# State-space mixer: the pooled product as one float32 matmul, outputs ahead of injections, low parts between parts of a rotation

## The chip, the cores and the metric

The kernel runs on one core of a Trainium2 chip. The metric is device time in microseconds (us) of one execution. Three executions of the kernel before gave 1857.22, 1857.31 and 1859.56 us; the median is 1857.31. Engines are called by their short names: PE (TensorE, matmuls), DVE (VectorE), ACT (ScalarE), POOL (GpSimd) and SP (SyncE, which here only issues DMAs).

## The reference

A trunk of two layers over 512 tokens of 1024 channels, in float32. The change touches one stage of layer 0, the mixer. Its input projection gives 512 pooling channels and 512 state-space channels.

```python
def pool_mixer(u, w_grp, scale):          # 4 groups of 128 channels, windows 2, 4, 8, 16
    ...
        outs.append((csg[:, end] - csg[:, start]) / cnt - uf[:, :, c0:c1])
    p = jnp.stack(outs, axis=2)
    y = jnp.einsum('blgc,gcd->blgd', p, w_grp.astype(F32)).reshape(bsz, L, D_POOL)
    return (y * scale.astype(F32)).astype(u.dtype)

def s5_mixer(u, a_re, a_im, log_dt, b_re, b_im, c_re, c_im, d_skip, w_glu, b_glu):
    ...
    y = jnp.transpose(y_f + y_b, (1, 0, 2, 3)).reshape(bsz, L, D_SSM) + d_skip.astype(F32) * uf
    y = jax.nn.gelu(y)
    y = y * jax.nn.sigmoid(y @ w_glu.astype(F32) + b_glu.astype(F32))
    return y.astype(u.dtype)
```

`y_f` and `y_b` come from a complex diagonal recurrence forwards and backwards over the tokens. The two halves of the mixer are joined and multiplied by one output matrix (1024 x 1024, `ab_w_out`).

## The kernel before, in words

**Products in parts.** Nearly every large product is three matmuls (`mm3`, L179 to L183): a float32 operand is kept as a high part (a cast by ACT) and a low part (operand minus high part, by DVE), and the three are high by high, low by high, high by low. A weight comes from memory as `w_raw` (two buffers), is cast by ACT to `w_hi` (L124) and its low part is taken by DVE as `w_lo` (L135). `take()` hands over the next weight, `done()` gives one back and starts the cast and low part of the next ones. All loads of weights and tables are issued by SP in program order. A result of PE is split on its way out by `split_evac`: high part by ACT (L399), low part by DVE (L400).

**The mixer's stage** is the 136 us from 405 to 541 us of the span. Its 512 state-space channels are worked in four tiles `ct`. For each: `inject(ct)`, 64 small float32 matmuls into the one buffer `ps_x` (L1433); `scan(ct)`, all on DVE: two products of `ps_x` with a rotation `ce` (L1451, L1452, the "first pair"), an addition and a subtraction (L1454, L1455), four recurrences (L1460), two more rotation products (L1462, L1463) and four combinations (L1468); `permute(ct)`, two copies by ACT; `output(ct)`, 96 small matmuls into `ps_y` (L1490, L1494), a gelu by ACT (L1497) and a write to memory (L1498, ACT's queue); `y_rows(ct)`, the read of it in another layout (L1502, SP's queue); `split_y(ct)` (L1506, L1507). `scan` is a generator: at each `yield` the program may place other work before DVE's next part.

**The pooling half** has four tiles too. `pool_tile(i)` projects 128 channels (24 matmuls into the one buffer `ps_p`), ACT copies them out twice (`pz`, `pp`), and POOL forms the window sums, corrects the edges and subtracts (L1526 to L1537). `rest()` splits the result (L1541 ACT, L1542 DVE) and `pool_out(i)` multiplies it by a 128 x 128 weight in three matmuls; tiles 0 to 2 use the three `ps_A` banks, tile 3 uses `ps_p`.

**The output product** `out_a` adds up into `psA[0..3]`: the first three take over the three `ps_A` banks, so each waits until the pooled result in its bank has been evacuated. It also works in row parts: pooled channels first (`kt` 0 to 3), state-space channels later. After the four `y` tiles have arrived comes `glu` (three-part products into `psG`), then the loop over `d` (sigmoid by ACT L1645, product by DVE L1646, split L1649 and L1650), then the rest of `out_a`, and `psB`, the second half of the output columns.

What sets the order on an engine is the program alone: each engine executes its own instructions in the order in which the code was written, and waits at an instruction until its inputs are there and its output buffer is free.

Of the kernel before, what the change touches and what calls it, by code (L numbers as in the profile page):

```python
# [7 lines left out]
F32 = mybir.dt.float32  # L8
F32R = mybir.dt.float32r
# [6 lines left out]
P = 128  # L16
# [157 lines left out]
class Builder:  # L174
# [1199 lines left out]
    def mixer(self, nxt, before):  # L1374
# [43 lines left out]
        yp = y = yhl = sp = us = edge = None  # L1418
# [18 lines left out]
        def decay(ct):  # L1437
            rho = con[ct, "rho"] = sp.tile([P, 2, 4, 64], F32, tag="rho", bufs=2, name="rho")
            for d in range(2):
                col = 16 * d + 4 * ct  # L1440
                nc.scalar.copy(rho[:, d], self.rho8[:, col:col + 4].unsqueeze(2).broadcast_to([P, 4, 64]))
                nc.scalar.mul(rho[:, d, :, 63 * d:63 * d + 1], rho[:, d, :, 63 * d:63 * d + 1], 0.0)

        def scan(ct):
# [17 lines left out]
            V.tensor_tensor(out=t2, in0=t1, in1=rot(1), op=ALU.mult)  # L1462
            V.tensor_tensor(out=t1, in0=t1, in1=rot(0), op=ALU.mult)  # L1463
# [40 lines left out]
        def split_y(ct):  # L1504
            hi, lo = (z[:, ct] for z in yhl)
            nc.scalar.copy(hi, y[:, ct])  # L1506
            V.tensor_tensor(out=lo, in0=y[:, ct], in1=hi.bitcast(F32), op=ALU.subtract)  # L1507

        def pool_tile(i):
# [41 lines left out]
        lhs = lambda kt: (xh[:, kt], xl[:, kt])  # L1551
# [10 lines left out]
        for i, win in enumerate(self.POOL_W):  # L1562
            G.tensor_scalar(out=scol[:, i:i + 1], in0=scol[:, i:i + 1], scalar1=1.0 / win, scalar2=None, op0=ALU.mult)
        rest = [pool_tile(0)]
        decay(0)
        decay(1)
# [4 lines left out]
        rest.append(pool_tile(1))  # L1571
        rest[0]()
        decay(2)
        inject(1)
        load("m3", "e2")
        for _ in scan(1):
            pass
        rest.append(pool_tile(2))
        rest[1]()
        permute(0)  # L1580
        decay(3)
        inject(2)
        load("i1", "g1")
        self.W.done()
        output(0)
        turn = scan(2)
        next(turn)
        rest[2]()
        self.W.done()
        y_rows(0)  # L1590
        load("e3", "g2")
        for _ in turn:
            pass
        rest.append(pool_tile(3))
        permute(1)
        inject(3)
        output(1)
        load("i2")
        y_rows(1)
        load("g3", "i3")  # L1600
        w_pool = self.W.take()
        for i in range(3):
            pool_out(i)
        turn = scan(3)
        next(turn)
        rest[3]()
        self.W.done()
        permute(2)
        out_a(range(3), range(2))
        next(turn)  # L1610
        pool_out(3)
        for _ in turn:
            pass
        output(2)
        permute(3)
        split_y(0)
        split_y(1)
        out_a(range(3), range(2, 4))
        y_rows(2)
        self.W.done(2)  # L1620
        output(3)
        y_rows(3)
        wide = self.bank("ps_x")
        psG = [wide[:, :512], wide[:, 512:], self.bank("ps_p")]
        wG = [self.W.take() for _ in range(2)]

        def glu(ds, kts):
            for kt, d in [(kt, d) for kt in kts for d in ds]:
                if d == len(psG):
                    psG.append(self.bank("ps_y"))  # L1630
                self.mm3(psG[d], [z[:, kt % 2 * HALF + d * P:kt % 2 * HALF + (d + 1) * P] for z in wG[kt // 2]],
                         [z[:, kt] for z in yhl], kt == 0, kt == 3)

        glu(range(3), range(2))
        split_y(2)
        glu((3,), range(2))
        out_a((3,), range(2))
        self.W.done()
        glu(range(4), (2,))
        split_y(3)  # L1640
        glu(range(4), (3,))
        out_a((3,), range(2, 4))
        for d in range(4):
            s = sp.tile([P, SEQ], F32, tag="yt", bufs=2, name="sg")
            nc.scalar.activation(out=s, in_=psG[d], func=AF.Sigmoid, bias=bcol[:, d:d + 1])  # L1645
            V.tensor_tensor(out=y[:, d], in0=y[:, d], in1=s, op=ALU.mult)  # L1646
            nat = lambda z: z[:, 4 + d].rearrange("p (c j) -> p j c", j=8)
            src = y[:, d].rearrange("p (j c) -> p j c", j=8)
            nc.scalar.copy(nat(xh), src)  # L1649
            V.tensor_tensor(out=nat(xl), in0=src, in1=nat(xh).bitcast(F32), op=ALU.subtract)  # L1650
            if d == 1:
                self.W.done()
        self.W.done(2)
# [29 lines left out]
    def mid_weights(self, ly):  # L1683
        w = self.ins
        if ly == 0:
            l = [w["w_in"][i] for i in (4, 5, 6, 7, 0, 1, 2, 3)] + [w["w_pool"]]
# [105 lines left out]
def lay_out(inputs):  # L1792
# [26 lines left out]
    edge = np.zeros((4, 16), np.float32)  # L1819
    for i, w in enumerate(Builder.POOL_W):  # L1820
        edge[i, :w // 2] = [w / (t + w // 2) for t in range(w // 2)]
        edge[i, 8:7 + w // 2] = [w / (w - 1 - k) for k in range(w // 2 - 1)]
# [17 lines left out]
        "w_pool": np.concatenate([a["pool_w"][0].transpose(1, 0, 2).reshape(P, HALF),  # L1840
                                  np.zeros((P, HALF), np.float32)], axis=1),
# [30 lines left out]
```

## Time and profile before

| | |
|---|---|
| median of 3 executions | 1857.31 us |
| profiled execution | 1861.19 us |
| its span on the core | 1859.3 us |
| granted TensorE clock, mean | 0.990 |
| PE busy | 97 % |
| DVE busy | 80 % |
| ACT busy | 50 % |
| POOL busy | 19 % |

The profiled execution is one execution with the hardware profiler on; the span is the part of it from the first to the last instruction, and 1.9 us lie outside. Busy shares are means over all stages. In the mixer's stage they are others, and the times in it are read from the engines' timelines (start and duration of each instruction, in us from the span's start).

### The profile page before, as it was taken

How to read it: one execution, taken by the hardware profiler on the slowest of the kernel's cores; microseconds unless marked ns; L12 is line 12 of the kernel's file. 1: busy time of each engine (PE TensorE's matmuls, PEld its weight loads, DVE VectorE, ACT ScalarE, POOL GpSimd, SP SyncE). 2: the span in 40 equal slices, each digit the busy share in tenths (PEclk: the TensorE clock that was granted, in tenths of full speed). 3: DMA queues.
4: the chain of work that ended last, by engine and by line, in shares of the span. 5: the costliest groups of instructions: out<-in, count | busy, mean ns of one | idle time of the engine just before them, and what ended most of it. 6: DMA issues, size and time to landing. Idle time of an engine off the chain costs nothing.

```text
span 1859.3 us, 31315 instructions
## 1 busy us (share of the span) xinstructions
PE 1798.2 (97%) x12144; PEld 1626.2 (87%) x12144; DVE 1486.4 (80%) x2396; ACT 935.7 (50%) x1769; POOL 360.9 (19%) x254
## 2 busy tenths in 40 slices
PE   8999999998899999999999999999999899999998
PEld 7887997787679999988899998889888789999886
DVE  6898989968769999854799997455887589999745
ACT  6254446355456444444644445346777464454532
POOL 1021321014111322300123221002333012223100
PEclk9999999999999999999999999999999899999999
DMA  5474346638532333232223333323333223332331
GB/s 198 137 222 165 103 135 193 207 123 261 176 114 81 102 113 103 92 125 92 90 92 103 113 103 115 101 69 109 112 110 105 89 80 103 103 111 95 125 102 58
DMA packets 88932, 224.42 MB, mean 121 GB/s; under 512 B 16560, under 2 KB 29008, under 8 KB 87760
## 3 DMA queue, kind: packets, MB, share of 16 engines
q1 hardware_dynamic: 77088, 196.75, 32.3%
q0 software_dynamic: 6960, 23.57, 4.2%
q10 hardware_dynamic: 4736, 2.10, 0.4%
q8 instruction: 96, 1.57, 0.4%
q14 instruction: 52, 0.43, 0.1%
HBM read 205.64 MB, written 18.84 MB: 121 GB/s over the span
## 4 chain that ended last, share of the span: by engine, by line
PE 59%; DVE 9%; ACT 3%; issue 2%; DMA 2%; POOL 0%; DVEq 0%; ACTq 0%; POOLq 0%
PE ps_gu L183 10%; PE ps_gu L182 10%; PE ps_gu L181 10%; PE ps_A L181 3%; PE ps_A L183 3%; PE ps_A L182 3%; PE ps_B L181 3%; PE ps_B L183 3%; PE ps_B L182 3%; PE ps_f L181 2%; PE ps_f L183 2%; PE ps_f L182 2%; DVE w_lo L135 2%; ACT junk L237 1%; PE ps_o L958 1%
## 5 line engine op out<-in xcount | busy, mean ns | idle before, releaser
L135 DVE TENSOR_TENSOR w_lo<-w_raw,w_hi 128x1024 fp32r<-128x1024 f32 x214 | 283.0, 1327 | 211.6 <-ACT w_hi L124 211.2
L124 ACT CAST w_hi<-w_raw 128x1024 fp32r<-128x1024 f32 (+1 forms) x313 | 262.9, 864 | 279.2 <-PE ps_A L183 74.1
L183 PE MATMUL ps_gu<-xsum,w_lo 128*128 128x256 f32 x1088 | 308.9, 284 | 0.8 <-DVE w_lo L135 0.8
L182 PE MATMUL ps_gu<-xsum,w_hi 128*128 128x256 f32 x1088 | 308.6, 284 | 0.8 <-DVE xsum L518 0.8
L183 PE MATMUL ps_gu<-xT_hi,w_lo 128*128 128x256 f32 (+1 forms) x1008 | 307.6, 305 | 1.7 <-DVE w_lo L135 1.7
L181 PE MATMUL ps_gu<-xsum,w_hi 128*128 128x256 f32 x1088 | 308.3, 283 | 0.0
L181 PE MATMUL ps_gu<-xT_hi,w_hi 128*128 128x256 f32 (+1 forms) x1008 | 304.9, 302 | 0.0
L182 PE MATMUL ps_gu<-xT_lo,w_hi 128*128 128x256 f32 (+1 forms) x1008 | 304.6, 302 | 0.0
L183 PEld LDWEIGHTS ps_gu<-xsum,w_lo 128*128 128x128 f32 x1088 | 209.4, 192 | 1.0 <-DVE w_lo L135 0.9
L182 PEld LDWEIGHTS ps_gu<-xsum,w_hi 128*128 128x128 f32 x1088 | 209.2, 192 | 1.0 <-DVE xsum L518 1.0
L181 PEld LDWEIGHTS ps_gu<-xsum,w_hi 128*128 128x128 f32 x1088 | 209.1, 192 | 0.0
L183 PEld LDWEIGHTS ps_gu<-xT_hi,w_lo 128*128 128x128 f32 x1008 | 190.4, 189 | 14.2 <-DVE w_lo L135 3.4
L181 PEld LDWEIGHTS ps_gu<-xT_hi,w_hi 128*128 128x128 f32 x1008 | 190.3, 189 | 8.5 <-issue 0.9
L182 PEld LDWEIGHTS ps_gu<-xT_lo,w_hi 128*128 128x128 f32 x1008 | 190.2, 189 | 7.3
L109 POOL TENSOR_TENSOR w_u<-w_raw,w_s 128x512 f32<-128x512 f32 x64 | 112.2, 1753 | 354.7 <-ACT w_hi L124 196.0
L124 ACT CAST w_hi<-w_s 128x512 fp32r<-128x512 f32 x136 | 77.8, 622 | 197.4 <-DVE w_s L105 197.4
L135 POOL TENSOR_TENSOR w_lo<-w_raw,w_hi 128x1024 fp32r<-128x1024 f32 x31 | 74.2, 2395 | 497.4 <-ACT w_hi L124 469.1
L105 DVE TENSOR_TENSOR w_s<-w_raw,w_u 128x1024 f32<-128x1024 f32 x68 | 145.8, 2144 | 2.3
L640 POOL TENSOR_TENSOR g<-g,m 128x1024 f32<-128x1024 f32 x34 | 94.6, 2782 | 244.9 <-DVE m L638 244.9
L181 PE MATMUL ps_B<-w_hi,gT 128*128 128x512 f32 x352 | 137.8, 391 | 2.0 <-DVE free L1303 2.0
L183 PE MATMUL ps_A<-w_hi,gT 128*128 128x512 f32 x352 | 137.7, 391 | 1.1 <-DVE gT L693 1.1
L181 PE MATMUL ps_A<-w_hi,gT 128*128 128x512 f32 x352 | 138.1, 392 | 0.0
(381 smaller groups left out, 4215.5 us busy)
## 6 DMA issues: line engine op xcount, KB each, us to landing
w_raw<-in_w_gu_dram SPq DMA_DIRECT2D x106, 512.0 KB, 3.4
w_raw<-in_w_dn_dram SPq DMA_DIRECT2D x88, 512.0 KB, 3.3
w_u<-in_w_gu_dram SPq DMA_DIRECT2D x70, 512.0 KB, 3.7
w_raw<-in_w_qk_dram SPq DMA_DIRECT2D x16, 512.0 KB, 3.4
w_raw<-in_w_in_dram SPq DMA_DIRECT2D x8, 512.0 KB, 3.4
cm<-m_dram SPq DMA_DIRECT2D x4, 1024.0 KB, 8.3
w_raw<-in_w_ao_dram SPq DMA_DIRECT2D x8, 512.0 KB, 3.8
cg<-g_dram SPq DMA_DIRECT2D x4, 1024.0 KB, 7.2
```

The source lines that it names most:

```text
L105: tt(out=blocks(s), in0=g[:, :HALF].unsqueeze(1).broadcast_to([P, 2, HALF]), in1=blocks(u)[:, :2], op=ALU.subtract)
L109: (h_engine or self.nc.gpsimd).tensor_tensor(out=z["h"], in0=g[:, HALF:], in1=z["s"][:, HALF:], op=ALU.add)
L124: self.nc.scalar.copy(hi[:, k:k + step], src[:, k:k + step])
L135: (engine or self.lo_engine).tensor_tensor(out=lo[:, :n], in0=src, in1=hi[:, :n].bitcast(F32), op=ALU.subtract)
L181: mm(ps, a[0], b[0], start=start, stop=False)
L182: mm(ps, a[0], b[1], start=False, stop=False)
L183: mm(ps, a[1], b[0], start=False, stop=stop)
L237: self.nc.scalar.activation(out=junk[:, :src.shape[-1]], in_=src, func=AF.Square, scale=scale, accum_out=out)
L640: nc.gpsimd.tensor_tensor(out=rows(f), in0=rows(f), in1=m, op=ALU.mult)
L958: nc.tensor.matmul(o[:, at:at + n], head[:, s], x[:, chunks[0]:chunks[-1] + 1].rearrange("p c n -> p (c n)"), start=s == 1 and i == 0, sto ...
```

## The change

The pooling weight is no longer a weight item with a low part: it becomes a plain float32 tile of half the size, loaded by POOL's queue. `pool_out` is then one float32 matmul, and no split of the pooled tile is needed ahead of it. Its result is split into tiles of its own (`pool_hi`, `pool_lo`, which held the split `y` before), and the low part (DVE) is put off in a list, `lows`, that the program empties between parts of `scan`. `y` is split into the tiles that held the pooled result. `scan` has one more `yield`, between its two last rotation products. The edge correction on POOL is one operation for a tile in place of up to two, and the scale of the four tiles one in place of four. The fifth weight of the queue (the first of `out_a`) is cast and split at the stage's start, as the pooling weight was. Finally the main order is written anew: `output(ct)` ahead of `inject(ct + 2)`, products of `out_a` between scans, and `psA[3]` in `ps_p`, where it was in `ps_y`.

```diff
+            w_pool = sp.tile([P, HALF], F32, name="w_pool")
+            G.dma_start(w_pool, ins["w_pool"])
...
             V.tensor_tensor(out=t2, in0=t1, in1=rot(1), op=ALU.mult)
+            yield
             V.tensor_tensor(out=t1, in0=t1, in1=rot(0), op=ALU.mult)
...
         def split_y(ct):
-            hi, lo = (z[:, ct] for z in yhl)
-            nc.scalar.copy(hi, y[:, ct])
-            V.tensor_tensor(out=lo, in0=y[:, ct], in1=hi.bitcast(F32), op=ALU.subtract)
+            self.split_evac(xh[:, ct], xl[:, ct], y[:, ct], None, lows)
...
-        def pool_out(i):
+            pooled.append(p)
+
+        def pool_out(i, later):
+
             ps = self.bank("ps_A" if i < 3 else "ps_p")
-            self.mm3(ps, [z[:, i * P:(i + 1) * P] for z in w_pool], [v[:, i] for v in yhl], True, True)
-            self.split_evac(xh[:, i], xl[:, i], ps, scol[:, i:i + 1])
+            nc.tensor.matmul(ps, w_pool[:, i * P:(i + 1) * P], pooled[i], start=True, stop=True)
+            self.split_evac(*(x[:, i] for x in yhl), ps, scol[:, i:i + 1], later)
...
-                    psA[t] = self.bank("ps_A" if t < 3 else "ps_y")
+                    psA[t] = self.bank("ps_A" if t < 3 else "ps_p")
...
+        W.fill(5)
+        G.tensor_tensor(out=scol, in0=scol, in1=edge[:, :, 16], op=ALU.mult)
         decay(0)
-        decay(1)
+        pool_tile(0)
         inject(0)
...
+        turn = scan(1)
+        next(turn)
+        pool_tile(2)
+        run_lows()
+        output(0)
+        inject(2)
+        W.hi()
+        pool_out(1, lows)
...
+        next(turn)
         decay(2)
+        run_lows()
+        pool_tile(3)
+        W.done(2, fill=False)
+        pool_out(2, lows)
+        out_a(range(3), range(2))
+        for _ in turn:
+            pass
+        permute(1)
+        load("e3", "i2")
+        split_next()
         turn = scan(2)
         next(turn)
+        run_lows()
+        W.hi()
+        output(1)
+        inject(3)
+        load("g3")
+        y_rows(1)
+        out_a(range(3), (2,))
+        pool_out(3, lows)
+        next(turn)
+        next(turn)
+        run_lows()
+        out_a(range(3), (3,))
+        out_a((3,), range(4))
+        W.done(2, fill=False)
         for _ in turn:
             pass
...
         turn = scan(3)
         next(turn)
+        run_lows()
+        split_next()
...
         glu(range(3), range(2))
+        permute(3)
+        for _ in turn:
+            pass
+        output(3)
+        y_rows(3)
...
-            if d == 1:
-                self.W.done()
```

What this does to the order is shown at three places. First PE, from the third pooled product on, with the numbers of the tiles. Before, `ps_A_4768` is the third pooled product and `ps_A_4791`, `ps_A_4795` and `ps_A_4799` are the first three accumulators of `out_a`; injection and output lie elsewhere.

```order
L181 MATMUL ps_A_4768<-y_hi_4090,w_hi_4533 128x512
L182 MATMUL ps_A_4768<-y_lo_4091,w_hi_4533 128x512
L183 MATMUL ps_A_4768<-y_hi_4090,w_lo_4534 128x512
L181 MATMUL ps_A_4791<-w_hi_4598,xT_hi_3665 128x512
L182 MATMUL ps_A_4791<-w_lo_4599,xT_hi_3665 128x512
```

Now `ps_A_4625` is the third pooled product and `ps_A_4636` is the accumulator that takes over its bank; six more products follow behind the last row shown, then the output of tile 1.

```order
L1542 MATMUL ps_A_4625<-pp_4466,w_pool_4097 128x512
L181 MATMUL ps_A_4628<-w_hi_4250,pool_hi_4090 128x512
L182 MATMUL ps_A_4628<-w_lo_4251,pool_hi_4090 128x512
L183 MATMUL ps_A_4628<-w_hi_4250,pool_lo_4091 128x512
L181 MATMUL ps_A_4632<-w_hi_4250,pool_hi_4090 128x512
L182 MATMUL ps_A_4632<-w_lo_4251,pool_hi_4090 128x512
L183 MATMUL ps_A_4632<-w_hi_4250,pool_lo_4091 128x512
L181 MATMUL ps_A_4636<-w_hi_4250,pool_hi_4090 128x512
```

The pooled product is one row for three, and the third accumulator now stands six matmuls behind the pooled product whose bank it takes, ahead of `output(1)`, `inject(3)`, nine more products and `pool_out(3)` on PE. The bank is free when the low part of `pool_out(2)` has been taken on DVE.

Second DVE, from the end of `scan(1)` to the start of `scan(3)` (`t_4591` and `t_4666` belong to `scan(2)`). Before:

```order
L135 TENSOR_TENSOR w_lo<-w_raw,w_hi 128x1024
L1451 TENSOR_TENSOR t_4591<-ps_x,ce 128x1024
L1452 TENSOR_TENSOR t_4592<-ps_x,ce 128x1024
L1542 TENSOR_TENSOR y_lo<-pp,y_hi 128x512
L135 TENSOR_TENSOR w_lo<-w_raw,w_hi 128x1024
L1454 TENSOR_TENSOR t_4591<-t_4591,t_4592 128x512
L1455 TENSOR_TENSOR t_4591<-t_4591,t_4592 128x512
L1460 SCALAR_TENSOR_TENSOR t_4591<-rho,t_4591 128x256 x4
L1462 TENSOR_TENSOR t_4592<-t_4591,ce 128x1024
L1463 TENSOR_TENSOR t_4591<-t_4591,ce 128x1024
L1468 TENSOR_TENSOR s<-t_4591,t_4592 64x8x64 x4
L400 SCALAR_TENSOR_TENSOR xT_lo<-ps_A,mix_scol,xT_hi 128x512 x3
```

Now:

```order
L135 TENSOR_TENSOR w_lo<-w_raw,w_hi 128x1024
L1453 TENSOR_TENSOR t_4666<-ps_x,ce 128x1024
L1454 TENSOR_TENSOR t_4667<-ps_x,ce 128x1024
L400 SCALAR_TENSOR_TENSOR pool_lo<-ps_A,mix_scol,pool_hi 128x512
L1456 TENSOR_TENSOR t_4666<-t_4666,t_4667 128x512
L1457 TENSOR_TENSOR t_4666<-t_4666,t_4667 128x512
L1462 SCALAR_TENSOR_TENSOR t_4666<-rho,t_4666 128x256 x4
L1464 TENSOR_TENSOR t_4667<-t_4666,ce 128x1024
L400 SCALAR_TENSOR_TENSOR pool_lo<-ps_p,mix_scol,pool_hi 128x512
L1466 TENSOR_TENSOR t_4666<-t_4666,ce 128x1024
L1471 TENSOR_TENSOR s<-t_4666,t_4667 64x8x64 x4
L1453 TENSOR_TENSOR t_4879<-ps_x,ce 128x1024
```

The three low parts that stood together behind `scan(2)` have moved ahead (two into `scan(1)`, the third behind the first pair of `scan(2)`), and that of `pool_out(3)`, which stood inside `scan(3)`, now stands inside `scan(2)`, between its two last rotation products. One low part of a weight and the splits of the pooled tiles (L1542) are gone from here.

Third SP's queue, at the last reads of `y`. Before:

```order
L1392 DMA ci<-i_dram 128x1024
L74 DMA w_raw<-in_w_glu_dram 128x1024
L1502 DMA y<-y_dram 128x512
L74 DMA w_raw<-in_w_ao_dram 128x1024 x2
L1502 DMA y<-y_dram 128x512
L74 DMA w_raw<-in_w_ao_dram 128x1024 x4
```

Now:

```order
L1505 DMA y<-y_dram 128x512
L1392 DMA ci<-i_dram 128x1024
L1505 DMA y<-y_dram 128x512
L74 DMA w_raw<-in_w_ao_dram 128x1024
L1505 DMA y<-y_dram 128x512
L74 DMA w_raw<-in_w_ao_dram 128x1024 x5
```

The last row of `y` (tile 3) has one weight load ahead of it where it had two; the second of them, the fourth row block of `out_a`'s weight, now stands behind it.

## Rows read from the trace of the kernel before

**Rows 1.** By windows: us, then busy time and instructions of each engine, clock, DMA share.

```profile
430.30:492.50 62.20, 47.87 (x614) 39.84 (x616) 61.33 (x67) 29.32 (x47) 22.85 (x27) 0.92 0.69 232
```

**Rows 2.** DVE's timeline: start, duration in us, line, what it writes from what.

```profile
430.31 1.22 DVE L1451 TENSOR_TENSOR t<-ps_x,ce 128x1024 f32<-128x1024 f32 x1 [3.48 <-PE ps_x L1433]
...
436.38 1.22 DVE L1462 TENSOR_TENSOR t<-t,ce 128x1024 f32<-128x1024 f32 x1
437.64 2.15 DVE L1463 TENSOR_TENSOR t<-t,ce 128x1024 f32<-128x1024 f32 x1
...
444.42 0.69 DVE L1542 TENSOR_TENSOR y_lo<-pp,y_hi 128x512 fp32r<-128x512 f32 x1
...
446.16 1.21 DVE L1452 TENSOR_TENSOR t<-ps_x,ce 128x1024 f32<-128x1024 f32 x1
...
458.71 0.69 DVE L1542 TENSOR_TENSOR y_lo<-pp,y_hi 128x512 fp32r<-128x512 f32 x1
...
463.71 2.10 DVE L135 TENSOR_TENSOR w_lo<-w_raw,w_hi 128x1024 fp32r<-128x1024 f32 x1
...
476.99 2.07 DVE L400 SCALAR_TENSOR_TENSOR xT_lo<-ps_A,mix_scol,xT_hi 128x512 fp32r<-128x512 f32 x3
...
478.98 1.21 DVE L1451 TENSOR_TENSOR t<-ps_x,ce 128x1024 f32<-128x1024 f32 x1
...
513.99 1.23 DVE L135 TENSOR_TENSOR w_lo<-w_raw,w_hi 128x1024 fp32r<-128x1024 f32 x1
```

**Rows 3.** PE's timeline; in brackets idle time before and what ended it.

```profile
436.18 2.08 PE L1433 MATMUL ps_x<-us,cm 128*64 128x64 f32 x64
...
447.48 3.54 PE L1433 MATMUL ps_x<-us,cm 128*64 128x64 f32 x64 [3.15 <-issue]
...
462.91 2.09 PE L1433 MATMUL ps_x<-us,cm 128*64 128x64 f32 x64 [3.19 <-issue]
...
477.80 0.80 PE L181 MATMUL ps_A<-w_hi,xT_hi 128*128 128x512 f32 x1 [7.71 <-DVE xT_lo L400]
...
525.12 0.40 PE L181 MATMUL ps_B<-w_hi,xT_hi 128*128 128x512 f32 x1
```

**Rows 4.** DMA issued between 423.7 and 425: queue, KB, us from issue to landing.

```profile
w_raw<-in_w_pool_dram SPq DMA_DIRECT2D x1, 512.0 KB, 5.2
```

**Rows 5.** ACT's timeline.

```profile
424.53 1.05 ACT L124 CAST w_hi<-w_raw 128x1024 fp32r<-128x1024 f32 x1 [1.25 <-DMA w_raw<-in_w_in_dram]
...
428.29 1.10 ACT L1520 COPY pz<-ps_p 128x512 f32<-128x512 f32 x1 [2.71 <-PE ps_p L183]
...
429.17 1.17 ACT L1521 ACTIVATE pp<-ps_p 128x512 f32<-128x512 f32 x1
...
430.11 0.43 ACT L1441 COPY rho<-rho 128x256 f32<-128x256 f32 x1
...
484.82 0.69 ACT L399 ACTIVATE xT_hi<-ps_p,mix_scol 128x512 fp32r<-128x512 f32 x1 [5.95 <-PE ps_p L183]
...
528.80 0.60 ACT L237 ACTIVATE junk<-ps_y 128x512 bf16<-128x512 f32 x1 [1.36 <-DVE fg L253]
```

**Rows 6.** POOL's timeline.

```profile
437.61 1.09 POOL L1526 TENSOR_TENSOR pz<-pz 128x543 f32<-128x543 f32 x1 [5.25 <-ACT pz L1520]
...
445.65 1.09 POOL L1526 TENSOR_TENSOR pz<-pz 128x543 f32<-128x543 f32 x1 [1.61 <-ACT pz L1520]
```

**Rows 7.** By windows again: output(2), and what followed PE's longest wait.

```profile
484.70:487.64 2.94, 2.94 (x97) 2.88 (x96) 2.94 (x6) 0.69 (x1) 0.00 (x0) 1.00 0.37 135
...
477.80:481.60 3.80, 3.80 (x9) 3.06 (x10) 3.80 (x5) 1.07 (x2) 0.00 (x0) 0.50 0.84 289
```

**Rows 8.** The chain that ended last, from the end of output(3).

```profile
495.89 5.58 DMA y_dram<-yt
...
501.48 2.65 DMA y<-y_dram
```

**Rows 9.** DMA issued between 459 and 484.

```profile
w_raw<-in_w_glu_dram SPq DMA_DIRECT2D x2, 512.0 KB, 3.4
```

More of the change, by code (lines that the diff above doesn't have):

```diff
@@ L1558, in out_a, with run_lows, split_next @@
                 if psA[t] is None:
-                    psA[t] = self.bank("ps_A" if t < 3 else "ps_y")
+                    psA[t] = self.bank("ps_A" if t < 3 else "ps_p")
                 self.rows(psA[t], lhs, kt, t, wA[kt // 2], kt % 2, kt == 0, kt == KT - 1)
-        for i, win in enumerate(self.POOL_W):
-            G.tensor_scalar(out=scol[:, i:i + 1], in0=scol[:, i:i + 1], scalar1=1.0 / win, scalar2=None, op0=ALU.mult)
-        rest = [pool_tile(0)]
+        pooled, lows = [], []
+        W = self.W
+        def run_lows():
+            while lows:
+                lows.pop(0)()
+        def split_next():
+            W.lo()
+            W.load_ahead()
+        W.fill(5)
+        G.tensor_tensor(out=scol, in0=scol, in1=edge[:, :, 16], op=ALU.mult)
         decay(0)
-        decay(1)
+        pool_tile(0)
         inject(0)
@@ L1570, in mixer @@
             pass
-        rest.append(pool_tile(1))
-        rest[0]()
-        decay(2)
-        inject(1)
-        load("m3", "e2")
-        for _ in scan(1):
-            pass
[L1578 to L1583, printed above, removed]
-        self.W.done()
-        output(0)
+        pool_tile(1)
+        W.done(2, fill=False)
+        decay(1)
+        permute(0)
+        inject(1)
+        pool_out(0, lows)
+        load("m3", "e2")
@@ L1586, in mixer @@
         turn = scan(2)
         next(turn)
[L1588 to L1591, printed above, removed]
+        run_lows()
[11 more added lines that the diff above has]
+        out_a((3,), range(4))
+        W.done(2, fill=False)
         for _ in turn:
             pass
-        rest.append(pool_tile(3))
@@ L1595, in mixer @@
[L1595 to L1603, printed above, removed]
+        decay(3)
+        permute(2)
+        load("i3")
+        split_y(0)
+        split_y(1)
+        W.hi()
+        output(2)
+        y_rows(2)
         turn = scan(3)
         next(turn)
[L1606 to L1622, printed above, removed]
+        run_lows()
+        split_next()
         wide = self.bank("ps_x")
-        psG = [wide[:, :512], wide[:, 512:], self.bank("ps_p")]
-        wG = [self.W.take() for _ in range(2)]
+        psG = [wide[:, :512], wide[:, 512:]]
@@ L1627, in glu @@
+        wG = []
         def glu(ds, kts):
             for kt, d in [(kt, d) for kt in kts for d in ds]:
+                if kt // 2 == len(wG):
+                    wG.append(W.take())
                 if d == len(psG):
@@ L1631, in glu @@
                 self.mm3(psG[d], [z[:, kt % 2 * HALF + d * P:kt % 2 * HALF + (d + 1) * P] for z in wG[kt // 2]],
-                         [z[:, kt] for z in yhl], kt == 0, kt == 3)
+                         [z[:, kt] for z in (xh, xl)], kt == 0, kt == 3)
         glu(range(3), range(2))
-        split_y(2)
[L1636 to L1639, printed above, removed]
+        permute(3)
[3 more added lines that the diff above has]
+        y_rows(3)
+        split_y(2)
+        split_next()
+        run_lows()
+        glu(range(3), (2,))
+        glu((3,), range(3))
+        W.done(fill=False)
+        W.fill(3)
         split_y(3)
+        run_lows()
         glu(range(4), (3,))
-        out_a((3,), range(2, 4))
+        W.done(fill=False)
+        W.fill(3)
         for d in range(4):
@@ L1817, in lay_out @@
     bias = bias.reshape(16, 4, P, 256).transpose(0, 2, 1, 3)
-    edge = np.zeros((4, 16), np.float32)
+    edge = np.ones((4, 17), np.float32)
     for i, w in enumerate(Builder.POOL_W):
         edge[i, :w // 2] = [w / (t + w // 2) for t in range(w // 2)]
-        edge[i, 8:7 + w // 2] = [w / (w - 1 - k) for k in range(w // 2 - 1)]
+        edge[i, 17 - w // 2:16] = [w / (w - 1 - k) for k in range(w // 2 - 1)]
+        edge[i, 16] = 1 / w
     lanes = lambda z: z.reshape(2, 16, 2, 64, -1).transpose(2, 3, 0, 1, 4).reshape(P, 32, -1)
```

34 lines of the change are left out of this document (14 added, 20 removed).

## The prediction

> **What bounds the kernel now.** Over the whole span PE is the busy engine, but the change lies in a stage where it isn't. The view by windows gives DVE 61.33 of the 62.2 us between 430.3 and 492.5, PE 47.87 [rows 1]: from the start of `scan(0)` to the end of `scan(3)` DVE has work without a break. The DVE timeline says where each scan stands: `scan(0)` starts at 430.31, `scan(3)` at 478.98 [rows 2]. PE waits beside it, 7.71 us before 477.80, and the releaser is DVE's last L400 [rows 3]. That wait costs nothing today, because DVE never waits for PE here; what it needs next had been done long before. Behind `scan(3)` the path is a chain through output, the write and read of `y`, `glu` and the `d` loop. So two questions decide: does DVE get less to do, and does it now have to wait for PE?
>
> **The start.** The first weight of `out_a` takes the pooling weight's place ahead of `scan(0)`. The load issued at 423.84 landed 5.2 us later [rows 4], at 429.0; a cast takes 1.05 [rows 5] and a low part 1.23 (513.99), so DVE is free at 431.3 where `scan(0)` started at 430.31 [rows 2]: +1.0. `scan(0)` itself takes 14.1 us (430.31 to 444.42 [rows 2]).
>
> POOL's sums cost DVE time. Of two like products in SBUF the one at 436.38 took 1.22 us and the next, at 437.64, 2.15 [rows 2]. POOL's additions at 437.61 and 445.65 [rows 6] stood beside the second of them and beside a product that reads PSUM (446.16), which stayed at 1.21. The Trainium skill (SBUF — State Buffer, "SBUF: two separate sides") has the port pair of VectorE and GpSimd as a lock held for a whole instruction, for which a VectorE operation with two SBUF inputs contends against a GpSimd one that reads SBUF; these rows agree.
>
> Which of DVE's operations POOL's sums fall beside now changes. Tile 0: `ps_p` comes free after the cast (430.1), the decay (430.11 and three pairs like it, 1.2 together) and the copies `pz` and `pp` (428.29 to 430.34, 2.05 [rows 5]), thus at 433.4, and its sums lie beside SBUF operations, where they lay beside PSUM reads. I add 0.8, a bit less than the one excess of 0.93 at 437.64 (bounds 0 and 1.3); `scan(0)` ends at 446.2.
>
> PE then does 24 projections (5.8: 430.34 to 436.18), an injection (2.08 [rows 3]), a pooled product (0.9, below) and 24 projections again. Tile 2 is full at 448.0, POOL's sums of it start at 449.1, not at 445.65 [rows 6], and lie wholly beside `scan(1)`'s SBUF operations: +1.5 (0 to 2.6). `scan(1)` took 13.7 (from 445.0, behind the L1542 of 444.42, to 458.71); with two L400 (1.3; three took 2.07 [rows 2]) and that 1.5 it ends at 462.7.
>
> **The float32 product.** No row shows one of 512 columns. Nearest are the 64 float32 matmuls of 64 columns in 2.08 us [rows 3]: eight of them make 512 columns, 0.26 us, or 0.52 if they ran two side by side; doubled, 1.04. The three matmuls that it replaces cost 0.7. I take 0.9; only the fourth lies on the path, so this is ±0.4 at most.
>
> **The wait that decides.** The third accumulator of `out_a` waits for the bank of `pool_out(2)`, and so for its L400, which now stands behind the first pair of `scan(2)`. DVE: `scan(1)` to 462.7, a low part 1.8 (2.10 beside POOL at 463.71, 1.23 alone), first pair 2.3, L400 0.7 [rows 2]: X = 467.5. PE has meanwhile done output 0 (2.94 [rows 7], to 451.0), injection 2, `pool_out(1)`, projections (459.8), `pool_out(2)` and six products (462.1): it waits 5.4 us. That alone is no loss. But behind the waiting matmul on PE stands what DVE needs next: twelve products 2.8, output 1 3.0, injection 3 2.1, nine products 2.1, `pool_out(3)` 0.9, then ACT's high part 0.69 (484.82 [rows 5]): 11.6.
>
> After an idle stretch PE may run slowly. After the 7.71 us the granted clock was 0.50 (1.2 GHz) for 3.8 us [rows 7]; after 3.15 us idle an injection took 3.54, after 3.19 us another took 2.09 [rows 3], the time of full speed. So it may cost 0 to 1.9; I take 1.0. The L400 of `pool_out(3)` can start at 480.1.
>
> DVE is there sooner. This L400 stands behind two additions, four recurrences and a rotation product. With the first pair these took 7.3 us in `scan(0)` (430.31 to 437.60 [rows 2]), less the pair 4.9, with POOL's last sums some 6: 473.5. So DVE waits about 7 us, where it never waited before. After it come L400 0.7, one rotation product 1.2 and combinations 2.8: `scan(3)` starts at 484.8, not at 478.98 [rows 2]: **+5.8**. Bounds: +1.8 with nothing from POOL (X = 464.5) and full speed, +8 with 1.9 lost and POOL's high ends.
>
> DVE's saving (four L1542, 2.7, and one low part, 1.2) is spent waiting. `scan(3)` has as much between its parts as before: two splits of `y` and a low part for one L1542, a low part and an L400, 2.6 each: 0.
>
> **After the scans.** Output 3 now follows a stretch in which PE idles: half speed for its 3 us or none of it, 0 to 1.6, **+0.8**. Then the tail of the last `y`. Its write took 5.58 us, beside two weight loads that SP had just issued, the read 2.65 [rows 8], and two splits 1.3: 9.6. Now one of these loads stands behind the read on SP. The write may then be as short as the read, 2.6; but the low part of that weight stands ahead of the last split of `y` on DVE: 2.6, 0.4 to the load's issue, 3.4 for it to land [rows 9], cast 1.05, low part 1.23, split 0.69, together 9.4. I take **0**; −2.8 if that load doesn't delay the split, +3.0 if it does and the write stays long. The cast and low part in the `d` loop (L135 at 513.99 [rows 2]) go: **−1.1**.
>
> **psB.** `psA[3]` moves into `ps_p`, and it is that bank's place that the first matmul of `psB` takes over, so it waits until ACT has squared `psA[3]` for the norm. Before, PE went into `psB` at 525.12 without a break [rows 3], and that square ended at 529.4, plus 0.2 to read it [rows 5]: 4.3 us that today lie under `psB`'s products. Behind that wait on PE stands all of `psB`, and PE is what bounds from there on. A weight's cast and low part that stood ahead of this square move, so I take **+3.0** (2.0 to 4.3).
>
> **Sum.** 5.8 + 0.8 + 0 − 1.1 + 3.0 = +8.5 us. The profiled execution took 1861.19, 3.9 above the median of 1857.31; the waits are the same in both, so I add 8.5 to the median: 1865.8. All low bounds: 1.8 + 0 − 2.8 − 1.1 + 2.0 = −0.1; all high: 8 + 1.6 + 3.0 − 1.1 + 4.3 = +15.8.
>
> **Rivals.** *A. DVE doesn't wait.* If `pool_out(3)`'s high part is ready when DVE gets to it, at 473.5, the wait for the bank costs nothing; that wants X plus 11.6 by then, X before 462. For it: DVE sheds 3.9 us, and PE waits without loss today. Against it: X is 464.5 even with nothing added by POOL. `scan(3)` would then start 0.7 sooner than before: −0.7 + 0.8 − 1.1 + 3.0 = +2.0, 1859.3, no change; with `psB`'s wait hidden as well −1.0, and with the short write −3.8, 1853.5, faster.
>
> *B. The small wait.* X = 464.5, full speed, `psB` 2.0: 1.8 + 0 + 0 − 1.1 + 2.0 = +2.7, 1860.0.
>
> *C. Every sum of POOL costs in full.* The bounds 1.3 and 2.6 in place of 0.8 and 1.5 put X 1.6 later: 1867.4. For it speaks 437.64, against it that `scan(1)` lost no more than one or two such excesses. This is what the lock of the Trainium skill's page SBUF — State Buffer (section above) would make of it; the trace bears it out for single pairs.
>
> *D. Slow all along.* 1.9 behind the bank, output 3 at half speed, the write as long as before with the load waited for: 8.5 + 0.9 + 0.8 + 3.0, 1870.5. For it speaks the clock at 477.8 [rows 7], against it the injection at 462.91 [rows 3].
>
> **How the numbers follow.** The forecast as it stands 0.52, A 0.16, B 0.12, C 0.10, D 0.10. About 0.2 % (3.7 us; 1853.6 to 1861.0) is what a measurement tells from no change. Slower: forecast, C, D and a little of B, 0.73; within: most of A and B, 0.19; faster: the end of A, 0.08. The forecast's own range is 1861.5 to 1870. Eight in ten reaches from within A to past D, 1857 to 1873.
>
> **What would show it.** In the new profile: PE idle some 5 us with L400 as releaser, ahead of a product into `ps_A`; DVE idle some 7 us ahead of the L400 of `ps_p`, released by ACT's L399; `scan(3)` starting near 485; PE idle 2 to 4 us ahead of the first `ps_B` matmul, released by L237; no weight split in the `d` loop. The prediction is wrong if DVE has no such idle time, or if the square of `psA[3]` is done before PE gets to `psB`.

## The result, and the profile after

The changed kernel took 1869.71 us (median of 4 executions, 1867.73 to 1872.89), the kernel before beside it 1857.88 (4 executions): ratio 1.0062, interval 1.0050 to 1.0075, slower by some 11.8 us. The forecast was 1865.8 in 1857 to 1873, slower with 0.73. The direction held and the time lies in the range; the loss came out 3.3 us larger than the 8.5 forecast, nearest to rival D's 1870.5. Ratios are of the kernel that ran beside the one named, and leave out two executions far off all others (3015.75 us of the kernel before, 6204.91 us of the run with four waits mended), which the medians below include.

The profiled execution has a span of 1867.5 us. It entered the mixer's stage at 411.12 (ACT's first copy to `zt`), the profiled one of before at 414.11; over all runs told here that point lay between 408.5 and 414.2 with the same code ahead of it. So the two are compared from that point on, which takes 3.0 us of chance out of the difference of the spans:

| from the stage's start, us | before | after | difference | forecast |
|---|---|---|---|---|
| `scan(0)` starts | 16.20 | 17.72 | +1.5 | +1.0 |
| `scan(1)` starts | 30.92 | 31.21 | +0.3 | +1.2 |
| `scan(2)` starts | 46.35 | 51.76 | +5.4 | +4.0 |
| `scan(3)` starts | 64.87 | 73.61 | +8.7 | +5.8 |
| gelu of output 3 | 81.15 | 91.32 | +10.2 | +6.6 |
| first sigmoid of the `d` loop | 92.97 | 102.93 | +10.0 | +6.6 |
| last split of the `d` loop ends | 107.12 | 115.78 | +8.7 | +5.5 |
| first product of `psB` | 111.01 | 122.24 | +11.2 | +8.5 |
| first square of the new `h` | 127.14 | 138.48 | +11.3 | +8.5 |

(`scan(1)`'s forecast is 446.2 less 445.0, the `scan(2)` one 464.5 less 460.5.) DVE's timeline of the changed kernel shows where the waits are; in brackets the idle time ahead of an instruction and its releaser:

```profile
428.84 1.22 DVE L1453 TENSOR_TENSOR t<-ps_x,ce 128x1024 f32<-128x1024 f32 x1
...
442.33 1.23 DVE L1453 TENSOR_TENSOR t<-ps_x,ce 128x1024 f32<-128x1024 f32 x1
...
446.98 2.43 DVE L1462 TENSOR_TENSOR_SCAN t<-rho,t 128x256 f32<-128x256 f32 x4
454.97 0.75 DVE L400 SCALAR_TENSOR_TENSOR pool_lo<-ps_A,mix_scol,pool_hi 128x512 fp32r<-128x512 f32 x1 [5.56 <-ACT pool_hi L399]
...
462.88 1.21 DVE L1453 TENSOR_TENSOR t<-ps_x,ce 128x1024 f32<-128x1024 f32 x1
...
465.15 0.73 DVE L400 SCALAR_TENSOR_TENSOR pool_lo<-ps_A,mix_scol,pool_hi 128x512 fp32r<-128x512 f32 x1
...
471.11 1.23 DVE L1464 TENSOR_TENSOR t<-t,ce 128x1024 f32<-128x1024 f32 x1
479.92 0.75 DVE L400 SCALAR_TENSOR_TENSOR pool_lo<-ps_p,mix_scol,pool_hi 128x512 fp32r<-128x512 f32 x1 [7.58 <-ACT pool_hi L399]
...
484.73 1.22 DVE L1453 TENSOR_TENSOR t<-ps_x,ce 128x1024 f32<-128x1024 f32 x1
```

Where DVE had no idle time between `scan(0)` and `scan(3)` [rows 1], it now has two long ones. The second, 7.58 us, is the one forecast (some 7). The first, 5.56 at the low part of `pool_out(1)`, is not in the prediction. PE's timeline, and by windows (engines as in [rows 1]) its clock behind two of its waits:

```profile
430.70 0.79 PE L181 MATMUL ps_p<-xT_hi,w_hi 128*128 128x512 f32 x1 [3.11 <-ACT pp L1522]
...
465.94 0.80 PE L181 MATMUL ps_A<-w_hi,pool_hi 128*128 128x512 f32 x1 [4.30 <-DVE pool_lo L400]
...
478.14 1.02 PE L1542 MATMUL ps_p<-pp,w_pool 128*128 128x512 f32 x2
...
533.36 0.50 PE L181 MATMUL ps_B<-w_hi,pool_hi 128*128 128x512 f32 x1 [2.40 <-ACT junk L237]
```

```profile
430.70:435.00 4.30, 4.30 (x10) 3.43 (x11) 4.27 (x6) 0.00 (x0) 2.28 (x5) 0.50 1.08 332
465.90:470.00 4.10, 4.06 (x10) 3.19 (x11) 4.10 (x5) 0.00 (x0) 2.73 (x3) 0.50 0.60 215
```

PE stands 3.11 us for `ps_p` (ACT freed it late), then runs at 0.50 of its clock (1.2 GHz), so that the projections of tile 1 take some 8.6 us against 5.8 before [rows 3, 5]; what follows on PE is late by about 6, the wait and the slow clock together. The wait for the third bank is 4.30 us where 5.4 was forecast, the one ahead of `psB` 2.40 where 2 to 4 was. The float32 product takes 1.02 us from its first start to its last end; its two records start 0.43 us apart, so in a stream it takes 0.86, and 0.9 was reckoned. ACT's timeline shows the start, the high part of `pool_out(1)` and the last `y`:

```profile
426.62 1.04 ACT L124 CAST w_hi<-w_raw 128x1024 fp32r<-128x1024 f32 x1 [4.12 <-DMA w_raw<-in_w_ao_dram]
...
428.65 1.07 ACT L1521 COPY pz<-ps_p 128x512 f32<-128x512 f32 x1
...
452.25 0.60 ACT L1500 ACTIVATE yt<-ps_y 128x512 f32<-128x512 f32 x1
...
453.30 1.05 ACT L124 CAST w_hi<-w_raw 128x1024 fp32r<-128x1024 f32 x1 [0.45 <-ACT yt L1500]
454.25 0.69 ACT L399 ACTIVATE pool_hi<-ps_A,mix_scol 128x512 fp32r<-128x512 f32 x1
...
509.59 1.05 ACT L124 CAST w_hi<-w_raw 128x1024 fp32r<-128x1024 f32 x1 [4.55 <-DMA w_raw<-in_w_ao_dram]
510.55 0.61 ACT L396 CAST xT_hi<-y 128x512 fp32r<-128x512 f32 x1
511.70 1.04 ACT L124 CAST w_hi<-w_raw 128x1024 fp32r<-128x1024 f32 x1 [0.54 <-DMA w_raw<-in_w_ao_dram]
512.76 1.28 ACT L1668 ACT_TABLE_LOAD   x1
514.05 0.69 ACT L1668 ACTIVATE sg<-ps_x,mix_bcol 128x512 f32<-128x512 f32 x1
```

The copy to `pz` stands behind a cast that waited for its load, and behind the decay. (The section on the change says that the pooling weight was cast and split at the stage's start as well. It was not: by the ACT and DVE timelines its cast stood at 454.46 and its low part at 459.32, so the cast ahead of `pz` is an addition of the change.) The high part that ended DVE's first wait, at 454.25, stood on ACT behind the gelu of output 0 and one more cast of a weight; its product had ended at 453.78 on PE. So PE's lateness reached DVE by way of output 0 and ACT, and no run moves that cast.

### The profile page after: what moved, and what is told of

It is laid out like the page before. It is cut to its first block, busy times and chain, and to the rows that moved or that the text cites. A ratio compares the mean times of both kernels' runs of the same rounds, so it can differ in the third digit from the quotient of the medians.

```text
span 1867.5 us, 31292 instructions
## 1 busy us (share of the span) xinstructions
PE 1802.2 (97%) x12140; PEld 1627.8 (87%) x12140; DVE 1479.9 (79%) x2391; ACT 932.6 (50%) x1764; POOL 357.0 (19%) x249
## 3 DMA queue, kind: packets, MB, share of 16 engines
q8 instruction: 96, 1.57, 0.3%
## 4 chain that ended last, share of the span: by engine, by line
PE 59%; DVE 8%; ACT 3%; issue 2%; DMA 1%; POOL 0%; ACTq 0%; DVEq 0%; SPq 0%; POOLq 0%
PE ps_gu L183 10%; PE ps_gu L182 10%; PE ps_gu L181 10%; PE ps_B L181 3%; PE ps_B L183 3%; PE ps_B L182 3%; PE ps_A L183 3%; PE ps_A L181 3%; PE ps_A L182 3%; PE ps_f L181 2%; PE ps_f L183 2%; PE ps_f L182 2%; DVE w_lo L135 2%; ACT junk L237 1%; ACT w_hi L124 1%
```

## The experiments

My theory was that the new waits are separate, all on the path, and each due to the order on one engine. The general rival was that PE's or POOL's work bounds the stage, so that a wait taken away comes back elsewhere. Stage means from the first copy to `zt` to the first square of the new `h`: 127.14 us before, 138.48 in the changed kernel. Medians of different rows compare only roughly, since the kernel before beside them moved by 1.7 us; the ratios are the better measure.

A stage is that of one profiled execution, and the changed kernel's was an unlucky one: behind the wait for `ps_p` its projections of tile 1 took 8.6 us. In four of the runs below whose order is the same up to `scan(2)` (the third, fourth, fifth and seventh row) they took 7.3 to 7.4, because the clock was low for less long, and `scan(2)` started at 50.14 to 50.39 after the stage's start, not at 51.76. In the second row they took 8.6 again, and `scan(2)` started at 51.75. So 1.4 to 1.6 us of a stage's difference to the changed kernel can be this alone.

| run | median, us | before beside it, us | ratio to before, interval | stage, us |
|---|---|---|---|---|
| first pooling tile ahead | 1868.02 | 1859.33 | 1.0047 (1.0029 to 1.0064) | 136.28 |
| low part of `pool_out(3)` later | 1865.45 | 1859.33 | 1.0031 (1.0018 to 1.0043) | 135.51 |
| first row block in `ps_p` | 1867.18 | 1859.33 | 1.0042 (1.0027 to 1.0057) | 134.26 |
| last `y` split first | 1871.71 | 1859.33 | 1.0067 (1.0050 to 1.0083) | 139.71 |
| `out_a` behind `pool_out(3)` | 1861.89 | 1859.62 | 1.0019 (1.0009 to 1.0028) | 128.53 |
| the same, low part of `pool_out(1)` later | 1860.96 | 1859.62 | 1.0007 (0.9996 to 1.0019) | 127.61 |
| weights filled in the loop | 1868.12 | 1859.62 | 1.0050 (1.0032 to 1.0067) | 135.50 |
| four mended together | 1856.49 | 1859.62 | 0.9975 (0.9963 to 0.9987) | 122.37 |
| the same, low parts of `y` later | 1855.32 | 1858.90 | 0.9979 (0.9969 to 0.9988) | 123.82 |
| float32 product alone, in the kernel before | 1857.42 | 1859.03 | 0.9991 (0.9982 to 1.0000) | 127.15 |

**The first pooling tile ahead of the cast and the decay.**

```diff
+        pool_tile(0)
         W.fill(5)
...
         decay(0)
-        pool_tile(0)
```

> The first pooling tile's projection and its two copies out of ps_p are issued ahead of the cast of out_a's first weight and of the decay, as in the kernel before; nothing else changes. My theory: the wait of 5.56 us on DVE for the low part of pool_out(1) comes from PE, which stood 3.1 us for ps_p at the start and then ran the next projections at half clock (8.6 us for 5.8). Both go, that DVE wait falls below 1 us, scan(2) starts 4.5 to 5.5 us sooner, and as the second DVE wait (7.6 us) stays as it is, the time is 1864 to 1865.5. Rival: PE's work bounds the stage; then the second wait grows by what the first loses, and the time stays at 1868.5 or above.

DVE's timeline of this run, and last the row of ACT that it waited for:

```profile
426.55 2.15 DVE L135 TENSOR_TENSOR w_lo<-w_raw,w_hi 128x1024 fp32r<-128x1024 f32 x1 [4.68 <-ACT w_hi L124]
...
432.22 4.13 DVE L1462 TENSOR_TENSOR_SCAN t<-rho,t 128x256 f32<-128x256 f32 x4
...
437.64 2.22 DVE L1466 TENSOR_TENSOR t<-t,ce 128x1024 f32<-128x1024 f32 x1
...
451.41 0.75 DVE L400 SCALAR_TENSOR_TENSOR pool_lo<-ps_A,mix_scol,pool_hi 128x512 fp32r<-128x512 f32 x1 [0.67 <-ACT pool_hi L399]
```

```profile
450.70 0.68 ACT L399 ACTIVATE pool_hi<-ps_A,mix_scol 128x512 fp32r<-128x512 f32 x1
```

PE's wait at the start is gone, its clock stays full (5.9 us for tile 1's projections), and DVE's wait falls from 5.56 to 0.67. That doesn't show the cause of the wait, though. From the stage's start, the high part comes 1.5 us sooner (41.58 against 43.12), but DVE gets to its low part 3.3 us later (41.62 against 38.28). The cast now stands behind the copies, `scan(0)` starts 1.8 later than in the changed kernel, and DVE's operations meet POOL's sums (4.13 for the recurrences where 2.43 was had alone, 2.15 and 2.22 for 1.23). So `scan(2)` starts at 50.22, 1.5 us sooner and not 4.5 to 5.5, which four other runs reach without this edit. The median, 1868.02, lies between what theory and rival said. Most of the fall of the wait is work that DVE now does in its place.

**The low part of `pool_out(3)` later**, in `scan(3)`.

```diff
         pool_out(3, lows)
-        next(turn)
-        next(turn)
-        run_lows()
-        out_a(range(3), (3,))
-        out_a((3,), range(4))
-        W.done(2, fill=False)
         for _ in turn:
...
         turn = scan(3)
         next(turn)
         run_lows()
+        out_a(range(3), (3,))
+        out_a((3,), range(4))
+        W.done(2, fill=False)
         split_next()
```

> The low part of pool_out(3) moves from inside scan(2) to behind the first pair of scan(3), and with it the 21 products of out_a that read it, behind output(2) on PE. My theory: the DVE wait of 7.58 us was on the path; it goes, scan(3) starts 6 to 8 us sooner, PE gives about 2 back by its later products: 1862.5 to 1865. Rival: the injection of tile 3, which stands on PE behind the same wait for the bank, holds scan(3) as well; scan(3) starts at most 3 us sooner and the time is 1867 or above.

`scan(3)` starts at 65.40, 8.2 us sooner: the wait was on the path. Its own rows show what is given back:

```profile
478.87 0.75 DVE L400 SCALAR_TENSOR_TENSOR pool_lo<-ps_p,mix_scol,pool_hi 128x512 fp32r<-128x512 f32 x1 [1.06 <-ACT pool_hi L399]
482.30 1.29 DVE L397 TENSOR_TENSOR xT_lo<-y,xT_hi 128x512 fp32r<-128x512 f32 x2 [2.69 <-ACT xT_hi L396]
```

DVE now waits within `scan(3)` for ACT, and 5.0 of the 8.2 us are left at the gelu of output 3. The time came 4.3 us lower, a little less than I expected.

**The accumulator of the first row block in `ps_p`.**

```diff
-                    psA[t] = self.bank("ps_A" if t < 3 else "ps_p")
+                    psA[t] = self.bank("ps_A" if t else "ps_p")
...
-        out_a(range(3), range(2))
+        out_a(range(1, 4), range(2))
```

and so on for the other calls, `out_a((3,), ...)` to `out_a((0,), ...)`.

> The accumulator of out_a that lies in ps_p is that of the first row block in place of the last, so that the first product of psB waits for a square that is taken early. Same products, same banks. My theory: the 2.40 us that PE idles ahead of the first psB product fall below 0.4 and the time is 2.0 to 2.4 lower, 1867.3 to 1867.7. Rival: a wait for the weight's cast stands right behind it, and the time is 1869 or above.

```profile
532.30 0.39 PE L181 MATMUL ps_B<-w_hi,pool_hi 128*128 128x512 f32 x1
```

No wait is left ahead of `psB`: from the loop's last split to it 3.88 us, as before (3.89), where the changed kernel took 6.46. The median is 2.5 lower, as expected; of the 4.2 us that the stage is shorter, 1.5 lie ahead of `scan(2)`, where the clock alone differs.

**The last `y` split ahead of the weights.**

```diff
-        W.done(fill=False)
-        W.fill(3)
         split_y(3)
         run_lows()
+        W.done(fill=False)
+        W.fill(3)
         glu(range(4), (3,))
```

> The split of the last y tile is issued ahead of the cast and low part of out_a's later weights on ACT and DVE. My theory: the split then follows the read of y alone, sigmoid starts 2.5 to 2.9 us sooner, and the time is 1866.8 to 1867.3. Rival: the weight's cast and low part were under the landing of y in other executions, or are missed later by out_a: 1869 or above.

```profile
505.94 0.62 ACT L396 CAST xT_hi<-y 128x512 fp32r<-128x512 f32 x1 [4.19 <-DMA y<-y_dram]
506.46 2.00 ACT L124 CAST w_hi<-w_raw 128x1024 fp32r<-128x1024 f32 x2
512.10 1.04 ACT L124 CAST w_hi<-w_raw 128x1024 fp32r<-128x1024 f32 x1 [3.64 <-DMA w_raw<-in_w_ao_dram]
513.16 1.28 ACT L1668 ACT_TABLE_LOAD   x1
514.45 0.69 ACT L1668 ACTIVATE sg<-ps_x,mix_bcol 128x512 f32<-128x512 f32 x1
```

My theory fell. `y` is split 7.2 us after its gelu, not 10.1, but the sigmoid stands on ACT behind a cast that waits 3.64 us for its load, and starts later than before the edit. It was the load of a weight that ended last here, not `y`. The time, 1871.71, is in the rival's range.

**The casts of those weights in the loop**, after that result.

```diff
         W.done(fill=False)
-        W.fill(3)
+        W.hi()
+        split_next()
         split_y(3)
...
         W.done(fill=False)
-        W.fill(3)
         for d in range(4):
...
             V.tensor_tensor(out=y[:, d], in0=y[:, d], in1=s, op=ALU.mult)
+            if d in (1, 2):
+                W.hi()
+                split_next()
```

> The casts and low parts of out_a's fourth weight and of psB's first move from ahead of the sigmoids into the d loop, between a tile's product and its split, where ACT and DVE wait for each other. My theory after the run with the split first, where the last y was split 4.4 us sooner and the sigmoid started no sooner: the sigmoid stood on ACT behind a cast whose load had not landed. It now starts 4 us sooner, the loop is at most 0.5 us longer, the time 1865.5 to 1866.5. Rival: the casts lengthen the loop by their own 1.1 us each and the products of out_a miss the weight: 1868 or above.

From the gelu of output 3 to the first sigmoid 9.46 us (11.61 in the changed kernel), the loop 13.14 (12.85): a gain of 1.9, half of what I expected. The time, 1868.12, is at the edge of the rival's range, so it doesn't show the gain. The first product of `psB` is 4.5 us sooner in this execution (1.6 of it ahead of `scan(2)`), but PE then ran slowly: 1.5 us are lost between it and the new `h`.

```profile
528.41 0.57 PE L181 MATMUL ps_B<-w_hi,pool_hi 128*128 128x512 f32 x1 [2.40 <-ACT junk L237]
528.78 0.63 PE L182 MATMUL ps_B<-w_lo,pool_hi 128*128 128x512 f32 x1
```

**`out_a` behind `pool_out(3)`**: all work stays; the products between the wait for the bank and `pool_out(3)` move behind it, and the wait with them.

```diff
         pool_out(2, lows)
-        out_a(range(3), range(2))
...
         output(1)
         inject(3)
...
-        out_a(range(3), (2,))
         pool_out(3, lows)
+        out_a(range(3), range(3))
```

> On PE, output(1), the injection of tile 3 and pool_out(3) now stand ahead of out_a's first 27 products; the bank wait and all work stay. This tells what made DVE wait 7.58 us: my theory, the products that stood between the freed bank and pool_out(3). Then DVE's wait at the low part of pool_out(3) is below 1 us, scan(3) starts 6 to 7.5 us sooner from the stage's start, nothing is given back on PE since the products fit under scan(2) and the first part of scan(3), and the stage ends 5.5 to 7.5 us sooner: 1862.5 to 1864.5. Rival: PE is the bound behind scan(2), the products are missed later by output(2) and glu, and no more than 3 to 4 us come back, as with the low part moved later: 1865.5 or above.

```profile
470.32 1.23 DVE L1464 TENSOR_TENSOR t<-t,ce 128x1024 f32<-128x1024 f32 x1
471.46 0.74 DVE L400 SCALAR_TENSOR_TENSOR pool_lo<-ps_p,mix_scol,pool_hi 128x512 fp32r<-128x512 f32 x1
```

DVE doesn't wait. `scan(3)` starts at 64.57, 9.0 us sooner than in the changed kernel; 1.4 of them lie ahead of `scan(2)`, where the clock alone differs, and 7.7 within `scan(2)`. The stage is 9.9 shorter and the time 7.8 lower. Nothing is given back behind it: the gelu of output 3 comes 10.4 sooner. That decides against the rival: the order on PE held DVE.

It doesn't tell the two parts of that order from each other. I had expected the wait for the bank to stay. It is gone as well: PE's only stand there is now 2.76 us ahead of output 1, for ACT's copies (`perm`). By the rows of the changed kernel, 14.0 us lay between the freed bank and DVE's low part, and the 21 products of `out_a` made up 7.4 of them. Without them the high part would have been ready some 0.2 us after DVE got there. Without the 4.30 us of standing alone it would still have waited some 3.3. That is an estimate from these rows; no run takes away one of the two alone.

**The same, and the low part of `pool_out(1)` behind `scan(1)`.**

```diff
         next(turn)
         decay(2)
-        run_lows()
         pool_tile(3)
...
         for _ in turn:
             pass
+        lows.pop(0)()
         permute(1)
```

> The same, and the low part of pool_out(1) is taken behind scan(1), not between its recurrences and rotations. My theory: the first DVE wait (2.6 to 5.6 us, by whether PE ran slowly at the start) is on the path too; it goes, scan(2) starts 2.5 to 5.5 us sooner than in the changed kernel, and the time is 1858.5 to 1861. Rival: as in the run with the first pooling tile ahead, the wait goes and scan(2) starts no sooner, because DVE's operations meet POOL's sums instead: 1862.5 to 1864.5, the same as without this move.

```profile
449.36 1.57 DVE L1457 TENSOR_TENSOR t<-t,t 128x512 f32<-128x512 f32 x1
450.85 4.37 DVE L1462 TENSOR_TENSOR_SCAN t<-rho,t 128x256 f32<-128x256 f32 x4
...
457.77 3.58 DVE L1471 TENSOR_TENSOR s<-t,t 64x512 f32<-64x512 f32 x4
```

The first wait is gone (2.46 us in the run ahead), and in this execution `scan(2)` starts no sooner, 50.48 against 50.39. The operations beside POOL's sums are longer, 1.57 and 4.37 for 0.69 and 2.43. The Trainium skill (SBUF — State Buffer, "SBUF: two separate sides") has the port pair that VectorE and GpSimd share as an exclusive lock: whichever comes second waits until the first is done. These rows agree. So a wait of DVE that is taken away can come back in longer operations beside POOL.

That it always comes back isn't shown. The next two runs (four mended together, and the same with the low parts of `y` later) have the same order up to `scan(2)`, and there it starts at 48.51 and 48.57, 1.8 to 1.9 us sooner than in the run ahead. Here `scan(1)` began 0.6 us later than there and POOL's sums fell beside more of it. The time, 1860.96, lies in my theory's range, and its interval overlaps with that of the run ahead. So this run alone decides for neither.

**Four mended together**: this order, the first row block in `ps_p`, and the casts in the loop.

> The last three together with the accumulator of the first row block in ps_p. My theory: the stage's four new waits are separate and add up: 7 (pool_out(3)), 3 to 5 (pool_out(1)), 4 (the cast ahead of the sigmoid) and 2.4 (psB), against 11.3 that the stage had become longer: 1852 to 1855, faster than the kernel before. Rival: PE's own work becomes the bound once the waits go, and half of it comes back: 1859 to 1862.

```profile
455.16 0.75 DVE L400 SCALAR_TENSOR_TENSOR pool_lo<-ps_A,mix_scol,pool_hi 128x512 fp32r<-128x512 f32 x1
...
456.96 1.22 DVE L1453 TENSOR_TENSOR t<-ps_x,ce 128x1024 f32<-128x1024 f32 x1
...
514.70 0.40 PE L181 MATMUL ps_B<-w_hi,pool_hi 128*128 128x512 f32 x1
```

The stage takes 122.37 us, 4.8 less than before; the times give a ratio of 0.9975 (0.9963 to 0.9987), 1856.49 against 1859.62. It beats both kernels, the one before by a quarter of a per cent. Against the changed kernel the stage is 16.1 us shorter, and its own rows say where: 3.3 ahead of `scan(2)` (1.4 of it the clock, 1.9 the low part of `pool_out(1)`), 6.8 within `scan(2)`, 0.8 from there to the gelu of output 3, 2.6 in the tail of `y` and the loop, 2.6 ahead of `psB`. The runs one by one give 15.3 (9.9 and 0.9 by the two orders, 1.9 in the tail and the loop, 2.6 ahead of `psB`), with the same 1.4 of the clock in the first. So the waits add up, and the rival is out. The time is a little above what I expected: the first wait gave 1.9 where I had 3 to 5, and the cast ahead of the sigmoid 2.6 where I had 4.

**And the low parts of `y` 0 and 1 behind `scan(3)`**, with the products of `glu` that read them behind `output(3)`.

> All four mended waits, and the low parts of y tiles 0 and 1, for whose high parts DVE stood 3.14 us between the first pair and the rest of scan(3), are taken behind scan(3), with the products of glu that read them behind output(3). My theory: that stand is on the path, scan(3) ends 2.5 to 3.1 us sooner and the time is 2 to 3 us below the run with all four, some 1853.5 to 1854.5. Rival: glu's products then stand ahead of the last y's and nothing is won: 1856 or above.

Nothing more was won: the ratio is 0.9979, the stage 1.5 us longer, and the time, 1855.32, lies between theory and rival. I had misplaced the 3.14 us: they lie behind `scan(3)`, where DVE waits for the next `y`.

**The float32 product alone**, in the order of before: `pool_out` as in the change, without `rest()` and without the weight's low part; the first of the four products ahead of the last projection.

> The kernel before with one part of the change alone: the pooled product is one float32 matmul, with no split of the pooled tiles and no low part of its weight; the first of the four stands ahead of the last pooling projection, and its evacuation and the order of everything else stay. My theory: DVE is the bound from scan(0) to scan(3) there, so what it sheds (three splits of 0.7 to 1.1 and a low part of 1.2 ahead of scan(3), one split in it) brings the end of scan(3) 2.5 to 4.5 us nearer and the time 2.5 to 4.5 us below that of the kernel before. Rival: the float32 product (1.02 us for 0.7) or a wait for its evacuation takes it back: less than 1 us either way.

`scan(2)` starts 1.4 us sooner, `scan(3)` 0.8, and the gelu of output 3 and all behind it at most 0.1. Of the 3.4 us shed ahead of `scan(3)` most comes back in longer operations beside POOL's sums. The last 0.8 are lost on PE ahead of output 3: the 18 products behind its wait for DVE took 6.97 us where they took 6.28, at half clock for longer. In this profile the rival holds. The time is 1.6 us below that of the kernel before (0 to 3.3 by the interval), between what theory and rival said, and decides for neither. (An earlier form, 1862.22 us, kept the third pooled tile in the place that the read of `y` 1 fills, so that its product waited for that read and then took `y` in the pooled tile's place; it says nothing of the question.)

## Why the prediction came out as it did

- **The wait that decides** was right in place, mechanism and about in size: DVE stood 7.58 us for `pool_out(3)` (forecast some 7), because of what was queued on PE at and behind the bank. Turning that order took 7.7 us off `scan(2)`.
- **The term that was mis-sized** is that one: `scan(3)` started 8.7 us later, not 5.8. Between the freed bank and the L400 lay 14.0 us (465.9 to 479.92), not 12.6: the first dozen products ran mostly at half clock and took 5.2 us, 2.3 over the 2.9 of full speed, where I took 1.0 and bounded it at 1.9. The rest, 1.4, lies ahead of it, in `scan(1)`.
- **The start** was wrong in its way, and near in its sum by luck. I had POOL's sums lengthen `scan(0)` by 0.8 and `scan(1)` by 1.5. `scan(0)` took 13.5, less than 14.1, and the recurrences of `scan(1)` took 2.43 undisturbed; instead DVE waited 5.56 for `pool_out(1)`. I had followed PE's lateness to `ps_p` (433.4 forecast, 433.7 on the same clock) but not let its clock fall there, nor followed the high part through ACT. The `scan(2)` that I forecast, 4.0 us later than before, is the 50.14 to 50.39 of the four runs with the same order, where the clock was low for less long. Rival C is out with it. The +1.0 of `scan(0)` itself rests on a pooling weight cast ahead of it, which the kernel before didn't do; +1.5 was measured.
- **After the scans**: output 3 +1.4 (0.8 forecast), the last `y` −0.2 (0), the loop −1.3 (−1.1), `psB` +2.6 (3.0). The tail of `y` came out as reckoned, through the weight that I had in the sum; that the sigmoid too stands behind a load, I had not seen.
- **Rivals**: A is out, since DVE waits; B too; D was right that the clock is slow more than once, not in the write of `y`, which was short.
- **A reading**: PE's 7.71 us before 477.80 ended with the first of the three low parts that begin at 476.99, not the last. Nothing in the sum rests on it.

Left open: when the clock falls behind a wait. In nine profiles PE stood 2.69 to 3.17 us ahead of tile 1's projections. In five the first matmul already took 0.79 or 0.80 us, the time of half clock. In three it took 0.50, and half clock came two to six matmuls later, as in the run with the first row block in `ps_p`:

```profile
433.35 0.50 PE L181 MATMUL ps_p<-xT_hi,w_hi 128*128 128x512 f32 x1 [2.70 <-ACT pp L1522]
...
435.25 0.63 PE L182 MATMUL ps_p<-xT_lo,w_hi 128*128 128x512 f32 x1
```

In one, after 2.93 us, it stayed full. The 24 projections took 8.6 us in two of the nine, 7.3 to 7.4 in six and 5.9 in one. The first matmul behind a wait therefore doesn't tell what the wait costs.

## What to carry to other kernels

Where a matmul waits for a bank, look at what stands behind it in PE's queue: the wait and the products behind it together may hold the engine that sets the pace, here by 7.7 us. Put what the pacing engine needs next ahead of accumulations that nobody waits for. Take a wait of an engine for a loss only after asking what it covers: DVE's idle time beside POOL's sums was worth 0 to 1.9 us of 2.5. And when a wait shrinks, look whether what it waited for came sooner, or the engine itself came later.

## What the runs showed of the hardware

A float32 matmul of 128 x 512 took 1.02 us at full clock from first start to last end, listed as two records that start 0.43 us apart, so 0.86 in a stream; the three parts that it replaces start 0.23 apart, 0.70 in a stream. A restart after 2.4 us of idle (ahead of `psB`) ran at half clock in two of seven executions and cost 1.5 us up to the new `h`; in the other five, the changed kernel's among them, it ran at full clock. After 2.7 to 3.2 us (ahead of tile 1's projections) the clock fell in eight of nine, and 24 products took 7.3 to 8.6 us for 5.9.
